# A two-layer diffusion trunk on one core: layer 1's gate brought into columns and spread again through DRAM, and three pieces of side work at other places

## The chip, the cores and the metric

The kernel is one program on one core of a Trainium2 chip. The time is that of the device from the launch to the end, in microseconds (us); lower is better. Beside the times there is one profiled execution, whose trace gives each instruction's start, its length and what it waited for.

## What is computed

A trunk of two layers over 256 latent and 256 context tokens of width 2048. Of the reference, cut to what matters here:

```python
shift, scale, gate = jnp.split(silu_c @ w_mod[l] + b_mod[l], 3, axis=-1)
h    = rmsnorm(x, g_pre[l]) * (1.0 + scale[:, None]) + shift[:, None]
proj = h @ w_in[l]                        # columns: gMLP u, v, gate; q, k, v, gate; Fourier x, gate
y    = mixer_branches(proj, latent_attn, ...)   # 3 branches, 8 attention heads
y    = rmsnorm(y @ w_out[l], g_post[l])
x    = x + gate[:, None] * y              # the context stream likewise, in layer 0 only
```

So each layer has one large projection in, an attention of eight heads and two other mixers, one projection out, and a gate of 2048 values that multiplies the normalised result. The gate is `silu(c) @ w_mod[l][:, 4096:6144] + b_mod`: a vector, of which each value belongs to a column of `y`.

## The kernel before, in words

**Precision and tiling.** All large products are made in halves of fp32: an operand is split into a high part (a cast, on ACT) and the rest (a subtraction, on DVE), and `mm3` (L487 to L490) adds three matmuls, high by high, low by high and high by low. Layer 1's input projection takes two per step (L604, L605). Weights come by `Stream` (L391 to L483): SP loads a piece of 128x1024 into `raw` (3 buffers), ACT casts `whi` (L456, 4 buffers), DVE subtracts `wlo` (L458, 4 buffers), three pieces ahead of their use.

**Stages in order.** Layer 0's modulation and projection; its attention heads and other branches, woven into the projection's columns; the projection out (to about 737 us); the boundary, where the new stream is made; layer 1's projection and attention; and `finish` (L1119 onward), the projection out of layer 1, in four blocks of 512 columns, c = 0 to 3, with 16 k-steps of six matmuls each (two token tiles by three), from about 1030 us.

**What sets the order.** PE's order is written by hand. Side work stands in a list, `Later` (L353 to L377), a clock of its own that each k-step of a product moves on (`later.tick`): a generator that yields 6.0 goes on when the clock has moved by 6.0, and what it then emits comes at that place in PE's order. One k-step of `finish` moves the clock by 1.296, a k-step with 512 columns by 0.648, one of layer 1's projection by 0.324. The orders on DVE, ACT, SP and POOL are the scheduler's; each engine works strictly in its order.

**The gate of layer 1.** `mod_gate1` (L280 to L296) makes the four blocks of 512 values on DVE: each block is an accumulator of 128x512 (tags `ctrh`, `ctrl`, `nstrh`, `nstrl` for c = 0 to 3), to which 16 instructions (L289, L291) add weight rows times a value of `silu(c)`, one per partition. The rows come by SP in loads of 512 KB, two instructions' worth each (L287, tile `mraw`, two buffers). What is left is a sum over the 128 partitions. `gate1(c)` (L298 to L310) does it on PE: two loads on SP bring the block's `b_mod` and `g_post` to all partitions (L302, 256 KB each, into `ws` and `bsb`); ACT and DVE split the accumulator (L505, L506); after `YG` = 6.5 of the clock two matmuls with a matrix of ones leave the sum in all partitions (L307); DVE adds and multiplies (L308, L309). `GATES` (L336) says at which k-step of which column block the task is put in the list. The result is read when a column block of `y` is taken out of PSUM (`evac`, L1170, for c < 3; `close`, L1183, for c = 3), after the block's last matmul.

**The other places.** `mod_four` (L264 to L268) makes four blocks of another modulation vector; its end, `mod_end` (L270 to L278: four small matmuls at L273, then eight small DVE instructions, L150 to L156, into `gg`), is put 45.0 of the clock behind. `x1_of` (L1262 to L1269) makes a block of the new latent stream: a multiplication on DVE and, from the fifth block on, an addition of `x0` by an accumulating DMA on GpSimd's queue; in layer 1's first column blocks it is called `NX` = 4 blocks ahead (L796 to L800). `attention` (L935 to L1003) does `rope` on a head's q (L925 to L927), splits it (L505, L506), and after `YQ` of the clock makes the scores (6.0 in layer 1); then the softmax on ACT and DVE, and after `YA` and `YB` the transposes and the products with v.

Of the kernel before, what the change touches and what calls it, by code (L numbers as in the profile page):

```python
# [7 lines left out]
F32 = mybir.dt.float32  # L8
# [3 lines left out]
ALU = mybir.AluOpType  # L12

P = 128
D = 2048
KT = D // P
# [50 lines left out]
def trunk_kernel(ctx: ExitStack, tc: tile.TileContext, xT, xhalf, cT, wss, wsl, wmod, win, wout0, wout1, const, vec, rows,  # L67
                 wmat, bs, sink, out):
    nc = tc.nc
    V, A, G, PE, DMA = nc.vector, nc.scalar, nc.gpsimd, nc.tensor, nc.sync  # L70

    pool = ctx.enter_context(tc.tile_pool(name="sb", bufs=1))
    psum = ctx.enter_context(tc.tile_pool(name="ps", bufs=1, space=bass.MemoryType.PSUM))
    W2K = 7
    cnt = [0]

    def sb(shape, dt, tag, bufs=1):
        cnt[0] += 1
        return pool.tile(shape, dt, tag=tag, bufs=bufs, name=f"{tag}_{cnt[0]}")

    def w2k(shape, dt=F32):
        return sb(shape, dt, "w2k", W2K)

    def mm_ps(name="mm"):
        cnt[0] += 1
        return psum.tile([P, 512], F32, tag="mm", bufs=6, name=f"ps_{name}_{cnt[0]}")

    def ms_ps(name="ms"):
        cnt[0] += 1
        return psum.tile([P, 512], F32, tag="ms", bufs=2, name=f"ps_{name}_{cnt[0]}")  # L90
# [36 lines left out]
    def cc(name):  # L127
        o, w = COFF[name]
        return cst[:, o - P:o - P + w]

    def vc(l, name):
        o, w = VOFF[name]
        return vecs[:, l, o:o + w]
# [8 lines left out]
    g1 = []  # L142

    def mod_cols(l, cb, ps8):

        what, j0 = cb // 4, (cb % 4) * 4
        b = vc(l, "bmod")[:, cb * 4:cb * 4 + 4].unsqueeze(2).to_broadcast([P, 4, 2])
        sl = slice(j0, j0 + 4)
        if what == 0:
            V.tensor_tensor(out=sh[l][:, sl], in0=ps8, in1=b, op=ALU.add)  # L150
        else:
            dst = (gs[l] if what == 1 else gg0)[:, sl]
            g = vc(l, "gpre" if what == 1 else "gpost")[:, sl].unsqueeze(2).to_broadcast([P, 4, 2])
            V.scalar_tensor_tensor(out=dst, in0=ps8, scalar=1.0 if what == 1 else 0.0, in1=b,
                                   op0=ALU.add, op1=ALU.add)
            V.tensor_tensor(out=dst, in0=dst, in1=g, op=ALU.mult)  # L156
# [83 lines left out]
    def mod_dve(l, cb, red):  # L240

        acc = sb([P, 2, 512], F32, "macc")
        for kg in range(4):
            for kk in range(4):
                if kk % 2 == 0:
                    w = sb([P, 2, 512], F32, "mraw", 2)
                    DMA.dma_start(w, wmod[(cb - 8) if l == 0 else 4 + cb, kg][:, kk:kk + 2])
                for s in range(2):
                    c = cs[:, kg * 4 + kk, s:s + 1]
                    if kg == 0 and kk == 0:  # L250
                        V.tensor_scalar(out=acc[:, s], in0=w[:, kk % 2], scalar1=c, scalar2=None, op0=ALU.mult)
                    else:
                        V.scalar_tensor_tensor(out=acc[:, s], in0=w[:, kk % 2], scalar=c, in1=acc[:, s],  # L253
                                               op0=ALU.mult, op1=ALU.add)
                if kk % 2 and (kg < 3 or kk < 3):
                    yield
        t = sb([P, 2, 512], F32, "mraw", 2)
        for s in range(2):
            V.transpose(t[:, s], acc[:, s])
            V.tensor_reduce(out=red[:, s], in_=t[:, s].rearrange("p (b j) -> p b j", j=32),  # L260
                            axis=mybir.AxisListType.X, op=ALU.add)
        yield

    def mod_four(l, cbs):  # L264
        red = sb([P, 4, 2, 16], F32, "red", 2)
        for i, cb in enumerate(cbs):
            yield from mod_dve(l, cb, red[:, i])
        later.add(mod_end(l, cbs, red), 45.0)  # L268

    def mod_end(l, cbs, red):  # L270
        ps = ms_ps("modc")
        for q in range(4):
            PE.matmul(ps[32 * q:32 * q + 32, 0:32], cc("selq"),  # L273
                      red.rearrange("p c s (j q) -> p c s j q", q=4)[:, :, :, :, q], start=True, stop=True,
                      tile_position=(0, 32 * q))
        for i, cb in enumerate(cbs):
            mod_cols(l, cb, ps[:, 8 * i:8 * i + 8].rearrange("p (s j) -> p j s", s=2))
        yield 0.0  # L278
# [19 lines left out]
    def gate1(c):  # L298

        r = [sb([P, 512], F32, tag) for tag in ("ws", "bsb")]  # L300
        for i in range(2):
            DMA.dma_start(r[i], rows[None, i, c * 512:(c + 1) * 512].to_broadcast([P, 512]))  # L302
        parts = split_into(w2k([P, 512], F32R), w2k([P, 512], F32R), g1[c])
        yield YG
        ps = ms_ps("gate")
        for i, t in enumerate(parts):
            PE.matmul(ps, state["ones"], t, start=i == 0, stop=i == 1)  # L307
        V.tensor_tensor(out=g1[c], in0=r[0], in1=ps, op=ALU.add)  # L308
        V.tensor_tensor(out=g1[c], in0=g1[c], in1=r[1], op=ALU.mult)  # L309
        yield 0.0  # L310

    def mod_rest():
# [21 lines left out]
    LOWC = 60  # L334
    YT = 3.0
    GATES = {2: 0, 14: 1}, {14: 2}, {12: 3}, {}  # L336
    YG = 6.5
    WARM = 4
    YH = 2.0
    NX, LATE = 4, 12  # L340
    YX, YC, YE = [2.4, 1.4, 1.8], 1.5, 5.0
    YQ, YA, YB = [5.5, 6.0], [10.0, 8.6], [3.8, 4.0]

    def pace():

# [31 lines left out]
    later = Later()  # L377
# [126 lines left out]
    def split_into(hi, lo, src):  # L504
        A.copy(hi, src)  # L505
        V.tensor_tensor(out=lo, in0=src, in1=hi.bitcast(F32), op=ALU.subtract)  # L506
        return hi, lo
# [128 lines left out]
    def layer(l):  # L636
# [5 lines left out]
        if last:  # L642
            a = sb([P, 4, 256], F32, "macc")
            c = [sb([P, 2, S], F32, f"kt{j}") for j in range(2)]
# [10 lines left out]
        def take(k, which=(0,)):  # L655

            for i in which:
                if k % (2, 4, 8)[i] == 0:
                    ws_[i] = W.next()

        def start_av(k, ts):
            avw = ws_[0]
            c = slice((k % 2) * 512, (k % 2 + 1) * 512)
            for t in ts:
                sl = slice(t * P, (t + 1) * P)
                mm3(av[t], h_of(l, k, sl), part(avw, c), k == 0, k == KT - 1)
# [129 lines left out]
        for i, (k0, nk) in enumerate(blocks if l else ()):  # L796
            for k in range(k0, k0 + nk):
                made = make_h(1, k, rbs[0], [0])
                if k + NX < KT:
                    x1_of(k + NX)  # L800
            if i == 0:
                with tc.issue_after(made[0].ins), tc.issue_after(made[1].ins):
                    state["late"]()
            take(k0, (0, 1))
            start_av(k0, range(nt))
            if nk == 2:
                start_au(k0)
                start_av(k0 + 1, range(nt))
            start_au(k0 + nk - 1)
# [208 lines left out]
        for h in range(len(au), 4):  # L1018
            ps = tunit1([0])[0] if last else tunit(n)
# [3 lines left out]
        for g in range(4):  # L1023
            ps = tunit1([0])[0] if last else tunit(n)
# [3 lines left out]
        for h in range(4):  # L1028
            ps = tunit1([0])[0] if last else tunit(n)
            gate(h, ps)  # L1030
        state["phase"] = f"cg{l}"
        for g in range(4):
            ps = tunit1([0])[0] if last else tunit(n)
# [24 lines left out]
        for h in range(8):  # L1058
            ps = tunit1([0])[0] if last else tunit(n)
# [3 lines left out]
        for h in range(8):  # L1063
            ps = tunit1([0])[0] if last else tunit(n)
# [69 lines left out]
    def finish():  # L1134
# [68 lines left out]
        for c in range(4):  # L1203
            pss = [mm_ps("y") for _ in range(2)]
            back = BACK if c == 3 else 0
            w = []
            for k in range(KT + back):
                if k < KT:
                    if k % 2 == 0:
                        w.append(W.next())  # L1210
                    products(c, k, 0, pss[0])
                if k == KT - 1:
                    evac(c, 0, pss[0])
                    if c == 3:
                        close(0, pss[0])
                if k >= back:
                    products(c, k - back, 1, pss[1])
                later.tick(PASS * 1024)
                if k in GATES[c]:
                    later.add(gate1(GATES[c][k]))  # L1220
            evac(c, 1, pss[1])
        close(1, pss[1])

# [38 lines left out]
    def x1_of(k):  # L1262

        o = yo[k][:, LAT]
        V.tensor_tensor(out=o, in0=o, in1=state["r0"], op=ALU.mult)
        if k < 4:
            V.tensor_tensor(out=o, in0=o, in1=x0s[0][:, k], op=ALU.add)
        else:
            G.dma_start(o, xhalf[0, k // 4][:, k % 4], accum_op=ALU.add)  # L1269
# [45 lines left out]
    with tc.manual_schedule(engines={EN.PE}):  # L1315
# [12 lines left out]
        for k in range(KT):  # L1328
            q = w2k([P, T])
# [3 lines left out]
            c = slice(32 * (k % 4), 32 * (k % 4) + 32)  # L1333
# [3 lines left out]
        row = w2k([P, T])  # L1337
# [6 lines left out]
        ps = ms_ps("rs")  # L1344
# [16 lines left out]
        make_h(0, 0, rb0, [0, 1], e)  # L1361
        list(e)
        layer(0)
        state["acc"] = out_proj()
        layer(1)
# [78 lines left out]
```

## Time and profile before

| what | value |
|---|---|
| median of 3 runs | 1134.23 us (1133.79 to 1134.24) |
| the profiled execution's own time | 1132.31 us |
| its span, first to last instruction | 1130.5 us |
| busy in the span: PE, DVE, ACT, POOL | 1122.0, 927.6, 528.5, 33.7 us |
| mean granted TensorE clock | 0.999 |

The page gives each engine's busy time, the span in 40 slices, the DMA queues, the chain of work that ended last, the costliest groups of instructions and the DMA issues. A row of a timeline has the start, the length, engine, line, operation, `out<-in` and the tile's shape; what stands in square brackets is the time that the engine stood idle before it, and what released it. Matmuls overlap in PE, so the distance between two starts is read, not their length.

### The profile page before, as it was taken

What the parts mean: (1) busy time and instruction counts of PE and PEld (TensorE: products, weight loads), DVE (VectorE), ACT (ScalarE), POOL (GpSimd) and SP (SyncE); (2) the same over time, 40 slices, a digit from 0 to 9 for tenths busy, and PEclk for the clock granted to TensorE, in tenths of its full rate; (3) what the DMA queues carried; (4) which work ended last, traced back from release to release, by engine and by line L of the source; (5) the groups of instructions that cost most, each with busy time, mean ns of one, the idle gap of its engine ahead of it and who ended that gap; (6) DMA issues with size and microseconds to landing.
All of it is one profiled execution on the core that took longest, in us unless ns stands there. A gap on an engine that the chain in (4) does not pass through costs nothing.

```text
span 1130.5 us, 16656 instructions
## 1 busy us (share of the span) xinstructions
PE 1122.0 (99%) x6117; PEld 921.5 (82%) x6117; DVE 927.6 (82%) x1649; ACT 528.5 (47%) x991; POOL 33.7 (3%) x41
## 2 busy tenths in 40 slices
PE   8999999999999999999999999999999999999998
PEld 3666788888888888888888888988888888888886
DVE  1578799989888788898999988397889789878883
ACT  5322433322235666642533334256665369857551
POOL 0000000000000000000000000030500000000000
PEclk9999999999999999999999999999999999999999
DMA  9999656566656344356556665276956686556972
GB/s 350 403 402 400 243 181 202 170 206 192 215 175 188 107 140 131 122 180 211 186 170 223 221 212 179 94 170 213 226 168 197 214 295 195 158 170 198 315 251 75
DMA packets 75250, 235.85 MB, mean 209 GB/s; under 512 B 8736, under 2 KB 13216, under 8 KB 75168
## 3 DMA queue, kind: packets, MB, share of 16 engines
q1 hardware_dynamic: 70992, 230.85, 61.4%
q0 software_dynamic: 4032, 3.67, 2.2%
q8 instruction: 48, 0.79, 0.3%
q14 instruction: 34, 0.28, 0.1%
q10 hardware_dynamic: 144, 0.26, 0.1%
HBM read 232.65 MB, written 2.10 MB: 208 GB/s over the span
## 4 chain that ended last, share of the span: by engine, by line
PE 96%; DVE 1%; ACT 1%; DMA 0%; issue 0%; SPq 0%; POOLq 0%; DVEq 0%; ACTq 0%
PE ps_t L488 15%; PE ps_t L490 15%; PE ps_t L489 15%; PE ps_t L604 10%; PE ps_t L605 5%; PE ps_v L1053 3%; PE ps_y L488 3%; PE ps_y L490 3%; PE ps_y L489 3%; PE ps_mod L181 2%; PE ps_av L488 2%; PE ps_av L489 2%; PE ps_av L490 2%; PE ps_tp L995 1%; PE ps_v L1054 1%; PE ps_au L488 1%
## 5 line engine op out<-in xcount | busy, mean ns | idle before, releaser
L456 ACT CAST whi<-raw 128x1024 fp32r<-128x1024 f32 (+1 forms) x209 | 216.4, 1037 | 320.6 <-PE ps_t L489 221.9
L488 PE MATMUL ps_t<-hh,whi 128*128 128x512 f32 (+1 forms) x752 | 290.6, 386 | 0.0
L490 PE MATMUL ps_t<-hh,wlo 128*128 128x512 f32 (+1 forms) x752 | 289.7, 385 | 0.0
L489 PE MATMUL ps_t<-hl,whi 128*128 128x512 f32 (+1 forms) x752 | 289.6, 385 | 0.0
L458 DVE TENSOR_TENSOR wlo<-raw,whi 128x1024 fp32r<-128x1024 f32 (+1 forms) x209 | 250.9, 1203 | 45.8 <-ACT whi L456 40.0
L253 DVE SCALAR_TENSOR_TENSOR macc<-mraw,cs,macc 128x512 f32<-128x512 f32 x360 | 250.0, 745 | 11.5 <-DMA mraw<-in_wmod_dram 11.2
L604 PE MATMUL ps_t<-hh,whi 128*128 128x512 f32 x512 | 184.9, 399 | 0.0
L490 PEld LDWEIGHTS ps_t<-hh,wlo 128*128 128x128 f32 x752 | 141.3, 188 | 28.5
L488 PEld LDWEIGHTS ps_t<-hh,whi 128*128 128x128 f32 x752 | 141.3, 188 | 26.9
L489 PEld LDWEIGHTS ps_t<-hl,whi 128*128 128x128 f32 x752 | 141.3, 188 | 26.4
L605 PE MATMUL ps_t<-hh,wlo 128*128 128x256 f32 x512 | 143.4, 280 | 0.0
L604 PEld LDWEIGHTS ps_t<-hh,whi 128*128 128x128 f32 x512 | 96.2, 188 | 21.5
L605 PEld LDWEIGHTS ps_t<-hh,wlo 128*128 128x128 f32 x512 | 96.6, 189 | 0.4
L570 ACT ACTIVATE hh<-w2k,sh 128x256 fp32r<-128x256 f32 x48 | 22.1, 503 | 72.7 <-DVE w2k L566 72.7
L488 PE MATMUL ps_y<-whi,hh 128*128 128x512 f32 x104 | 41.3, 397 | 0.0
L490 PE MATMUL ps_y<-whi,hh 128*128 128x512 f32 x104 | 40.6, 390 | 0.0
L489 PE MATMUL ps_y<-wlo,hh 128*128 128x512 f32 x104 | 40.5, 389 | 0.0
L488 PE MATMUL ps_av<-whi,hh 128*128 128x512 f32 x94 | 39.0, 415 | 0.6 <-ACT hh L570 0.6
L489 PE MATMUL ps_av<-wlo,hh 128*128 128x512 f32 x94 | 37.1, 395 | 0.0
L505 ACT CAST w2k<-ps_tp 128x512 fp32r<-128x512 f32 x40 | 23.4, 586 | 20.3 <-PE ps_scc L489 8.6
L518 POOL TENSOR_TENSOR rs_b<-rs_a,mhalf 128x2 f32<-128x2 f32 (+1 forms) x6 | 6.6, 1096 | 776.8 <-DVE mx L1245 584.8
L506 DVE TENSOR_TENSOR w2k<-ps_tp,w2k 128x512 fp32r<-128x512 f32 x40 | 27.4, 684 | 1.3 <-ACT w2k L505 0.5
(458 smaller groups left out, 1777.0 us busy)
## 6 DMA issues: line engine op xcount, KB each, us to landing
raw<-in_win_dram SPq DMA_DIRECT2D x160, 512.0 KB, 4.1
mraw<-in_wmod_dram SPq DMA_DIRECT2D x128, 512.0 KB, 4.2
raw<-in_wout_dram SPq DMA_DIRECT2D x60, 512.0 KB, 4.4
mraw<-in_wsl_dram SPq DMA_DIRECT2D x14, 512.0 KB, 7.2
yo<-in_xT_dram SPq DMA_DIRECT2D x16, 256.0 KB, 5.3
yo<-in_wsl_dram SPq DMA_DIRECT2D x16, 256.0 KB, 7.2
macc<-in_wsl_dram SPq DMA_DIRECT2D x7, 512.0 KB, 7.7
vv<-in_wsl_dram SPq DMA_DIRECT2D x7, 512.0 KB, 8.4
```

The lines of the kernel that those rows point to most:

```text
L181: PE.matmul(self.ps[32 * kk:32 * kk + 32, 0:self.N], cpad[:, kg * 4 + kk], self.w[kg * 4 + kk], start=kg == 0, stop=kg == 3, tile_position ...
L253: V.scalar_tensor_tensor(out=acc[:, s], in0=w[:, kk % 2], scalar=c, in1=acc[:, s], op0=ALU.mult, op1=ALU.add)
L456: A.copy(ph, rc)
L458: self.last = V.tensor_tensor(out=pl, in0=rc, in1=ph.bitcast(F32), op=ALU.subtract)
L488: PE.matmul(ps, st[0], mv[0], start=start, stop=False)
L489: PE.matmul(ps, st[0], mv[1], start=False, stop=False)
L490: PE.matmul(ps, st[1], mv[0], start=False, stop=stop)
L505: A.copy(hi, src)
L506: V.tensor_tensor(out=lo, in0=src, in1=hi.bitcast(F32), op=ALU.subtract)
L604: PE.matmul(ps, w[0], h, start=k == 0, stop=False)
L605: PE.matmul(ps[:, 0:S], w[1], h[:, 0:S], start=False, stop=k == KT - 1)
L1053: PE.matmul(vps[t], hi, wk, start=k == 0, stop=False)
```

## The change

It has four parts. Blocks 1, 2 and 3 of layer 1's gate go another way (block 0 stays with `gate1`). `MODEND` puts layer 0's `mod_end` 8 of the clock further behind. `AHEADX` makes the calls of `x1_of` run up to two blocks further ahead in layer 1's first steps. `YQ` of layer 1 goes from 6.0 to 6.8.

```diff
-        later.add(mod_end(l, cbs, red), 45.0)
+        later.add(mod_end(l, cbs, red), MODEND[l])
...
         parts = split_into(w2k([P, 512], F32R), w2k([P, 512], F32R), g1[c])
-        yield YG
+        yield YG[0]
...
+    def gate1_dram(c):
+
+        tag = ("ctrh", "ctrl", "nstrh", "nstrl")[c]
+        red, t = sb([P, 16], F32, "red", 2), w2k([P, 512])
+        V.transpose(t, g1[c])
+        V.tensor_reduce(out=red, in_=t.rearrange("p (b j) -> p b j", j=32), axis=mybir.AxisListType.X, op=ALU.add)
+        yield YG[1]
+        ps = ms_ps("gate")
+        for q in range(4):
+            PE.matmul(ps[32 * q:32 * q + 32, 0:4], cc("selq"), red.rearrange("p (j q) -> p j q", q=4)[:, :, q],
+                      start=True, stop=True, tile_position=(0, 32 * q))
+        col = sb([P, 4], F32, "mx", 2)
+        V.tensor_tensor(out=col, in0=ps[:, 0:4], in1=vc(1, "bmod")[:, 32 + 4 * c:36 + 4 * c], op=ALU.add)
+        V.tensor_tensor(out=col, in0=col, in1=vc(1, "gpost")[:, 4 * c:4 * c + 4], op=ALU.mult)
+        row = dram.tile([4, P], F32, tag=f"gate{c}", name=f"gate{c}")
+        with nc.allow_non_contiguous_dma(reason="512 values"):
+            G.dma_start(row.rearrange("j p -> p j"), col)
+        g1[c] = sb([P, 4, P], F32, tag)
+        G.dma_start(g1[c], row[None].to_broadcast([P, 4, P]))
+        g1[c] = g1[c].rearrange("p j f -> p (j f)")
+        yield 0.0
...
-    YG = 6.5
+    YG = 6.5, 3.0
+    MODEND = 53.0, 45.0
     WARM = 4
     YH = 2.0
-    NX, LATE = 4, 12
+    NX, AHEADX, LATE = 4, 2, 12
     YX, YC, YE = [2.4, 1.4, 1.8], 1.5, 5.0
-    YQ, YA, YB = [5.5, 6.0], [10.0, 8.6], [3.8, 4.0]
+    YQ, YA, YB = [5.5, 6.8], [10.0, 8.6], [3.8, 4.0]
...
-                if k + NX < KT:
-                    x1_of(k + NX)
+                for kk in range(min(2 * k, k + AHEADX) + NX, min(2 * k + 2, k + 1 + AHEADX) + NX):
+                    if kk < KT:
+                        x1_of(kk)
...
-                    later.add(gate1(GATES[c][k]))
+                    later.add((gate1_dram if GATES[c][k] else gate1)(GATES[c][k]))
```

The lines of the changed kernel are shifted: its L292 is L291 of before (the accumulation), L482 is L458 (`wlo`), L529 and L530 are L505 and L506 (the splits), L1195 is L1170 (`evac`), L950 to L952 are L925 to L927 (`rope`), L480 is L456 (`whi`).

The first place is on DVE in `finish`, late in column block 1 and at its `evac`, before the change; `nstrl` is block 3's accumulator, `nstrh` block 2's, the `mraw` tiles are the weight rows.

```order
L291 SCALAR_TENSOR_TENSOR nstrl_10269<-mraw_10444,cs_86,nstrl_10269 128x512 x2
L291 SCALAR_TENSOR_TENSOR nstrl_10269<-mraw_10472,cs_86,nstrl_10269 128x512
L458 TENSOR_TENSOR wlo_10531<-raw_10528,whi_10530 128x1024
L1170 TENSOR_TENSOR yo_1956_10547<-ps_y_10355,ctrl_8568 128x512
L506 TENSOR_TENSOR w2k_10559<-nstrh_9229,w2k_10558 128x512
L291 SCALAR_TENSOR_TENSOR nstrl_10269<-mraw_10472,cs_86,nstrl_10269 128x512
L458 TENSOR_TENSOR wlo_10571<-raw_10568,whi_10570 128x1024
L1170 TENSOR_TENSOR yo_1962_10562<-ps_y_10356,ctrl_8568 128x512
```

The same place on DVE with the change, from the fifth load of block 3 (`mraw_10449`) on:

```order
L292 SCALAR_TENSOR_TENSOR nstrl_10271<-mraw_10449,cs_88,nstrl_10271 128x512 x2
L482 TENSOR_TENSOR wlo_10496<-raw_10493,whi_10495 128x1024
L292 SCALAR_TENSOR_TENSOR nstrl_10271<-mraw_10477,cs_88,nstrl_10271 128x512 x2
L482 TENSOR_TENSOR wlo_10514<-raw_10511,whi_10513 128x1024
L292 SCALAR_TENSOR_TENSOR nstrl_10271<-mraw_10517,cs_88,nstrl_10271 128x512 x2
L482 TENSOR_TENSOR wlo_10536<-raw_10533,whi_10535 128x1024
L317 STREAM_TRANSPOSE w2k_10560<-nstrh_9231 128x512
L292 SCALAR_TENSOR_TENSOR nstrl_10271<-mraw_10539,cs_88,nstrl_10271 128x512
L1195 TENSOR_TENSOR yo_1956_10552<-ps_y_10353,ctrl_10409 128x512
L318 TENSOR_REDUCE red_10559<-w2k_10560 128x16
```

Before, the split of `nstrh` stood behind half of block 3's sixth load (`mraw_10472`); now the transposition and the reduction of `nstrh` stand behind block 3's sixth, seventh and half its eighth load (`mraw_10477`, `mraw_10517`, `mraw_10539`).

The second place is on PE: where gate 2's matmuls stand among those of column block 2 is given by the clock, and moves from six k-steps after that block's begin to three. For gate 1, in column block 1, the rows of PE with the change are:

```order
L512 MATMUL ps_y_10353<-whi_10296,hh_1847_10080 128x512
L513 MATMUL ps_y_10353<-wlo_10297,hh_1847_10080 128x512
L514 MATMUL ps_y_10353<-whi_10296,hh_1847_10080 128x512
L512 MATMUL ps_y_10354<-whi_10296,hh_1847_10080 128x512
L513 MATMUL ps_y_10354<-wlo_10297,hh_1847_10080 128x512
L514 MATMUL ps_y_10354<-whi_10296,hh_1847_10080 128x512
L322 MATMUL ps_gate_10399<-red_10345,cst_81 32x4 x4
L512 MATMUL ps_y_10353<-whi_10296,hh_1848_10083 128x512
```

The four small matmuls (32x4) take the place of two of 128x512, 22 rows earlier.

The third place is on DVE in layer 0's attention. Before, `mod_end`'s eight instructions stood ahead of a head's `rope` (L925 to L927) and of its splits (L506):

```order
L971 RECIPROCAL den_3400<-den_3400 128x4
L154 SCALAR_TENSOR_TENSOR gg_31_98<-ps_modc_3474,vecs_78 128x8 x2
L156 TENSOR_TENSOR gg_31_98<-gg_31_98,vecs_78 128x8
L154 SCALAR_TENSOR_TENSOR gg_31_98<-ps_modc_3474,vecs_78 128x8
L156 TENSOR_TENSOR gg_31_98<-gg_31_98,vecs_78 128x8
L154 SCALAR_TENSOR_TENSOR gg_31_98<-ps_modc_3474,vecs_78 128x8
L156 TENSOR_TENSOR gg_31_98<-gg_31_98,vecs_78 128x8
L925 TENSOR_TENSOR w2k_3441<-ps_t_3323,cst_79 128x256
L926 TENSOR_TENSOR mgl_2843<-mgl_2843,cst_79 128x256
```

With the change they stand behind the next head's probabilities, ahead of the head after:

```order
L996 RECIPROCAL den_3532<-den_3532 128x4
L530 TENSOR_TENSOR w2k_3570<-ps_tp_3564,w2k_3569 128x512
L155 SCALAR_TENSOR_TENSOR gg_31_100<-ps_modc_3615,vecs_80 128x8 x2
L157 TENSOR_TENSOR gg_31_100<-gg_31_100,vecs_80 128x8
L155 SCALAR_TENSOR_TENSOR gg_31_100<-ps_modc_3615,vecs_80 128x8
L157 TENSOR_TENSOR gg_31_100<-gg_31_100,vecs_80 128x8
L155 SCALAR_TENSOR_TENSOR gg_31_100<-ps_modc_3615,vecs_80 128x8
L157 TENSOR_TENSOR gg_31_100<-gg_31_100,vecs_80 128x8 x2
L950 TENSOR_TENSOR w2k_3588<-ps_t_3451,cst_81 128x256
```

The same moves on PE: `mod_end`'s four matmuls stand 62 matmuls later than before. On ACT, in layer 1's third head, the cast of q's high part stands behind one `whi` cast before the change (L456, then L505), and behind two with it (L480 twice, then L529).

More of the change, by code (lines that the diff above doesn't have):

```diff
@@ L73, in trunk_kernel @@
     psum = ctx.enter_context(tc.tile_pool(name="ps", bufs=1, space=bass.MemoryType.PSUM))
+    dram = ctx.enter_context(tc.tile_pool(name="dram", bufs=1, space=bass.MemoryType.DRAM))
     W2K = 7
```

## The prediction

> **What bounds the kernel now.** I read the page first: busy time by engine, then the chain that ended last, then the list of what PE waited for.
>
> ```profile
> PE 1122.0 (99%) x6117; PEld 921.5 (82%) x6117; DVE 927.6 (82%) x1649; ACT 528.5 (47%) x991; POOL 33.7 (3%) x41
> PE 96%; DVE 1%; ACT 1%; DMA 0%; issue 0%; SPq 0%; POOLq 0%; DVEq 0%; ACTq 0%
> ```
>
> ```profile
> PE ps_idle L533 <- DVE red L112: 2.0, 1, 2.0
> PE ps_av L488 <- ACT hh L570: 0.6, 1, 0.6
> PE ps_sc L490 <- DVE w2k L506: 0.6, 2, 0.4
> PE ps_x L1194 <- ACT w2k L1186: 0.5, 1, 0.5
> PE ps_rs L1334 <- ACT w2k L1330: 0.3, 1, 0.3
> ```
>
> PE is busy 1122.0 of 1130.5 us and makes up 96% of the chain. So an edit can gain only by taking matmuls away or by removing one of PE's few waits, and it loses by making PE wait. Of the waits listed the change can touch one: the scores (`ps_sc`), twice. The first, third, fourth and fifth are the start of the program and of its stages, and the tail. The two places of the scores, in PE's timeline:
>
> ```profile
> 371.95 0.60 PE L995 MATMUL ps_tp<-identr,w2k 128*128 128x128 f32 x4
> 372.63 0.50 PE L488 MATMUL ps_sc<-kt,w2k 128*128 128x512 f32 x1
> ...
> 373.56 0.50 PE L490 MATMUL ps_sc<-kt,w2k 128*128 128x512 f32 x1 [0.19 <-DVE w2k L506]
> 373.90 0.39 PE L488 MATMUL ps_sc<-kt,w2k 128*128 128x512 f32 x1
> ...
> 936.19 0.39 PE L489 MATMUL ps_sc<-ws,w2k 128*128 128x512 f32 x1
> 936.96 0.50 PE L490 MATMUL ps_sc<-kt,w2k 128*128 128x512 f32 x1 [0.38 <-DVE w2k L506]
> ```
>
> A 128x512 matmul in a row of them takes 0.23 us of PE (the chain's row at 1043.35, below). From 372.63 to 373.90 three intervals take 1.27, 0.58 too much; the four transposes ahead take 0.68, where the four of the row at 1042.92 take 0.44, so 0.24 too much. Together 0.8 us in layer 0. In layer 1 one interval of 0.77 is 0.54 too long.
>
> **The change, part by part.**
>
> *Layer 0's `mod_end`, 8 of the clock later.* Why the scores waited:
>
> ```profile
> 369.91 0.24 DVE L154 SCALAR_TENSOR_TENSOR gg<-ps_modc,vecs 128x8 f32<-128x8 f32 x2 [3.44 <-PE ps_modc L273]
> ...
> 385.13 0.43 DVE L925 TENSOR_TENSOR w2k<-ps_t,cst 128x256 f32<-128x256 f32 x1 [2.97 <-ACT mgl L923]
> ```
>
> DVE stood 3.44 us until PE had made `mod_end`'s sums, and the head's `rope` and splits queued behind. With the change that wait is gone, and `mod_end`'s eight small instructions come about 12 us later, into DVE's idle 2.97 us before 385.13, where nothing is delayed. What is late next: the high half on ACT, which now comes as early as its own copies allow. I take the whole gain, -0.8 us; the bounds are -0.8 and, if ACT and DVE in the next heads, whose order moves too, make one score wait as long as layer 1's does, -0.8 + 0.5 = -0.3.
>
> *Layer 1's scores at 6.8.* The scores stand two steps of the projection later, 6 matmuls or 0.69 us by the pace above. But the order on ACT changes as well: two `whi` casts, not one, stand before the cast of q's high half.
>
> ```profile
> 933.94 1.05 ACT L456 CAST whi<-raw 128x1024 fp32r<-128x1024 f32 x1
> 935.39 0.41 ACT L505 CAST w2k<-mgl 128x256 fp32r<-128x256 f32 x1 [0.41 <-DVE mgl L927]
> ```
>
> A cast takes 1.05, and the second needs the weight buffer that PE frees at about 935.9. So the high half is ready at 935.9 + 1.05 + 0.41 = 937.4, not 935.8, while PE asks at 935.93 + 0.69 = 936.6: a wait of 0.8 where there was 0.54. Against this, DVE's low half (L506, which ended the old wait) has 0.69 more. I take 0.0; bounds -0.5 (the wait gone) and +0.8 (one more such wait in a later head, since the whole chain of a head shifts by two steps).
>
> *`AHEADX`.* The same multiplications and transfers, some earlier.
>
> ```profile
> 738.30 7.37 POOL L1269 DMA_DIRECT2D yo<-in_xhalf_dram  x8 [4.02 <-DVE w2k L566]
> ```
>
> POOL issues the first eight transfers in one run, 0.92 us each, so its own pace sets when they land; earlier calls on DVE don't bring them forward by much. PE shows no wait at that place. 0.0; bounds -0.3 and +0.3, a third of one issue each way.
>
> *Gates on PE.* Three times two 128x512 matmuls go and four small ones (eight in the trace) come.
>
> ```profile
> 1044.34 0.39 PE L490 MATMUL ps_y<-whi,hh 128*128 128x512 f32 x1
> 1044.57 0.62 PE L307 MATMUL ps_gate<-w2k,join 128*128 128x512 f32 x2
> 1045.03 0.40 PE L488 MATMUL ps_y<-whi,hh 128*128 128x512 f32 x1
> ...
> 130.65 0.40 PE L490 MATMUL ps_av<-whi,hl 128*128 128x512 f32 x1
> 130.97 0.24 PE L193 MATMUL ps_modc<-w2k,cst 128*32 128x4 f32 x8
> 131.15 0.50 PE L488 MATMUL ps_au<-hh,whi 128*128 128x512 f32 x1
> 131.49 0.40 PE L489 MATMUL ps_au<-hl,whi 128*128 128x512 f32 x1
> ```
>
> ```profile
> 1042.92 0.44 PE ps_x L1147 x4
> 1043.35 0.23 PE ps_y L488
> ```
>
> The old pair costs 1045.03 - 1044.34 - 0.23 = 0.46 us. The small group of the same shape (32x4) at 130.97 stretches the two intervals around it from 0.46 to 0.84: 0.38 us. So a gate saves 0.08, three save 0.24. I take -0.2. The removed ACT casts and DVE work lie beside PE and gain nothing by themselves.
>
> *Gate 2's place.* This is the main term. PE comes to gate 2's matmuls three k-steps after column block 2 begins, 18 matmuls, and no longer six.
>
> ```profile
> 1077.82 0.39 PE L488 MATMUL ps_y<-whi,hh 128*128 128x512 f32 x1
> ...
> 1085.98 0.63 PE L307 MATMUL ps_gate<-w2k,join 128*128 128x512 f32 x2
> ```
>
> With 1077.82 as the block's begin that is 1077.82 + 18 x 0.2275 = 1081.9. What it needs is DVE's reduction of `nstrh` (L318). In DVE's new order that stands behind block 3's loads up to the first half of the eighth, P7 (P0 to P7 are the loads of `mraw` for that block). Before, half of P5 was enough. DVE works in order, so the reduction can't be done before P7 has landed, and with two buffers P7 is asked for only when P5 is used up, P5 when P3, P3 when P1.
>
> ```profile
> 1061.55 0.74 DVE L291 SCALAR_TENSOR_TENSOR nstrl<-mraw,cs,nstrl 128x512 f32<-128x512 f32 x1
> ...
> 1063.34 0.74 DVE L291 SCALAR_TENSOR_TENSOR nstrl<-mraw,cs,nstrl 128x512 f32<-128x512 f32 x1
> ...
> 1083.00 0.68 DVE L1170 TENSOR_TENSOR yo<-ps_y,ctrl 128x512 f32<-128x512 f32 x1
> 1083.60 1.22 DVE L458 TENSOR_TENSOR wlo<-raw,whi 128x1024 fp32r<-128x1024 f32 x1
> ...
> 1086.88 0.75 DVE L291 SCALAR_TENSOR_TENSOR nstrl<-mraw,cs,nstrl 128x512 f32<-128x512 f32 x1 [0.61 <-DMA mraw<-in_wmod_dram]
> ```
>
> ```profile
> q1 hardware_dynamic: 4396, 14.93, 89.3%
> ...
> mraw<-in_wmod_dram SPq DMA_DIRECT2D x10, 512.0 KB, 5.4
> ```
>
> The last fence is the DMA view of 1040 to 1090: the 16 engines are 89.3% busy there, and a load of `mraw` takes 5.4 us to land. Before, the two rows at 1061.55 and 1063.34 are P1, used up at 1064.0; without the longer additions of gate 1 ahead I put it at 1063.3. Then P7 lands three landings and two uses (2 x 0.7 each) later: 1063.3 + 3 x (5.4 + 0.1) + 2 x 1.4 = 1082.6. Behind it stand half of P7 (0.67), `evac` (0.60, from 1083.00 to 1083.60) and the reduction, which I put at the 0.60 that a 512-wide instruction takes there: 1084.5. **PE waits 1084.5 - 1081.9 = 2.6 us.** Queued behind it is all of block 2. The bounds: with 4.2 us per landing, the page's median for `mraw`, P7 lands at 1079.0 and nothing waits;
>
> ```profile
> mraw<-in_wmod_dram SPq DMA_DIRECT2D x128, 512.0 KB, 4.2
> ```
>
> at before's pace P7 is only there at 1086.88 (the row above is its first half), the reduction ends at 1088.8, and PE waits 6.9. I choose 5.4, the value of this very stage: two row loads leave the queues, but two loads of weights must come sooner.
>
> Gates 1 and 3 I cost at nothing. Gate 1's reduction stands behind fewer loads and, by the same rows, about 1 us ahead of PE's place (1058.8), a margin that one late load can take; gate 3's accumulator is complete some 10 us ahead of its place.
>
> *The way through DRAM.* DVE's two tiny instructions, a transfer of 512 single values out and one of 256 KB back. It is read at `evac`, 20 us or more after the matmuls for blocks 1 and 2. For block 3 there is less, since it is read at `close`:
>
> ```profile
> 1102.78 0.63 PE L307 MATMUL ps_gate<-w2k,join 128*128 128x512 f32 x2
> ...
> 1117.52 0.68 DVE L1183 TENSOR_TENSOR yo<-ps_y,nstrl 128x512 f32<-128x512 f32 x1
> ```
>
> That is 14.7 us from the old place, and the new one is some k-steps ahead of it: 17 us. The nearest row for the transfers is `x0`'s transfers on the same queue; two, one after another, each as long as the whole run of eight at 738.30 (7.4 us), are 15 us. That is covered. If the cover were gone, `evac` would come late, but PE has a second pair of accumulators to go on with, and the cost shows only at the last block. 0; bounds 0 and +3.2, for what its packets take from the loads:
>
> ```profile
> q0 software_dynamic: 4032, 3.67, 2.2%
> ```
>
> This row of the page gives 0.022 x 16 x 1130.5 / 4032 = 0.099 us of an engine per packet; 512 packets are 51 us of one engine or 3.2 us of all sixteen, and they come when P2 or P3 is on its way. A rule of the Trainium skill speaks against the change here: by "DMA: Bandwidth & Descriptors", section "Rules for kernel authors", a strided transfer becomes one descriptor per element. By that the write has 512 packets and costs as said, +3.2 at most; no run here shows it yet.
>
> **Sum, against the profiled execution:** -0.8 + 0.0 + 0.0 - 0.2 + 2.6 = +1.6 us, so 1132.3 + 1.6 = 1133.9. The profiled execution lies 1.9 us below the median of the runs; I add the difference to the median: 1134.2 + 1.6 = **1135.8 us**.
>
> **The rivals.**
>
> *No wait at gate 2 (faster side).* The loads land in 4.2 to 4.7 us, since four rows' loads less are in the way. At 4.7, P7 lands at 1080.5 and the wait is 0.5. For it: the 89.3% includes those rows. Against: no load of the stage landed under 4.7. Total: -0.8 - 0.2 = -1.0, and with layer 1's wait gone as well -1.5: 1132.7. Only with a gain at `AHEADX` or beside it does it pass -2.3.
>
> *The chain of loads is slower (slower side).* The 512 packets and the denser loads add 3.2 us before P7: PE waits 5.8 at gate 2, up to the 6.9 of before's pace. Total +4.8: 1139.0. It passes +2.3 from a wait of 3.3 at gate 2 on, a mean landing of 5.6 us.
>
> *The scores don't gain.* The later places move the waits without removing them (-0.3 and +0.8 in place of -0.8 and 0.0): +2.9, 1137.1.
>
> *The change doesn't do what it says.* The gates were to relieve PE and don't: 0.24 us. That is already in the sum.
>
> **How the numbers follow.** Chances: the forecast (a wait of 1 to 4 us at gate 2) 0.47; no wait 0.23; slower loads 0.20; scores without gain 0.10. The range reaches from the end of the second case with a little more, 1132.0, to 1139.8, that is the third case with its wait at 6.6. About 0.2%, 2.3 us, is what a measurement of this kernel can tell from no change. Faster by more than that needs the second case and a gain that I can't name: 0.11. Slower by more than 1136.5 are the third case, two thirds of the fourth, and the upper third of the forecast: 0.42. The rest, 0.47, lies within.
>
> **What would show it.** Right: PE's list of waits shows `ps_gate` behind DVE's `red` at 1081.9, 1 to 4 us, once; DVE idles ahead of it for `mraw`; the scores near 372 start 0.23 apart; `ps_sc` near 937 still waits 0.5 or more, for ACT. Wrong: no wait of `ps_gate`, a wait for weights (`wlo`) in `finish`, one at `evac` for the transfer back, or new waits of the scores in layer 0's heads from 398 on.

## The result and the profile after

The change made the kernel slower: 1146.39 us (1143.9 to 1147.59, 4 runs) beside 1134.01, a ratio of 1.0106, interval 1.0094 to 1.0118. The forecast was 1135.8, and the range ended at 1139.8. The profiled execution took 1146.76 us with a span of 1145.0, where before had 1132.31 and 1130.5.

PE's waits in the changed kernel, the longest first (us in total, times, longest):

```profile
PE ps_gate L322 <- DVE red L318: 5.2, 1, 5.2
PE ps_y L513 <- DVE wlo L482: 4.1, 1, 4.1
PE ps_idle L557 <- DVE red L113: 2.0, 1, 2.0
PE ps_x L1219 <- ACT w2k L1211: 1.7, 1, 1.7
PE ps_av L512 <- ACT hh L594: 0.6, 1, 0.6
PE ps_sc L512 <- ACT w2k L529: 0.4, 1, 0.4
```

The first wait is the one that was forecast, twice as long. The second, for weights in `finish`, is one that the prediction named as a sign that it is wrong, and the fourth has grown by 1.2. Matching PE's rows of both traces one by one shows where the time goes. At 1074.81 the changed kernel lies 0.3 us **ahead**. At the second matmul of column block 2 it lies 5.7 behind, ten matmuls past gate 2 13.2 behind, at the last product 13.3; the tail adds 1.2, and that is the 14.5 of the spans. PE's timeline at the two places:

```profile
1074.81 0.39 PE L512 MATMUL ps_y<-whi,hh 128*128 128x512 f32 x1
1079.30 0.50 PE L513 MATMUL ps_y<-wlo,hh 128*128 128x512 f32 x1 [4.11 <-DVE wlo L482]
...
1080.37 0.63 PE L514 MATMUL ps_y<-whi,hh 128*128 128x512 f32 x1
1080.80 0.63 PE L512 MATMUL ps_y<-whi,hh 128*128 128x512 f32 x1
...
1087.40 0.39 PE L514 MATMUL ps_y<-whi,hh 128*128 128x512 f32 x1
1092.96 0.29 PE L322 MATMUL ps_gate<-red,cst 128*32 128x4 f32 x8 [5.17 <-DVE red L318]
...
1094.20 0.63 PE L514 MATMUL ps_y<-whi,hh 128*128 128x512 f32 x1
1094.62 0.63 PE L512 MATMUL ps_y<-whi,hh 128*128 128x512 f32 x1
```

Behind each wait the starts lie 0.43 us apart instead of 0.23, for some 3 us. The windows show it as clock: in this view (us, busy time and count of PE, PEld, DVE, ACT and POOL, granted clock, DMA share, GB/s) the third number from the end is 0.66 and 0.57 around those places and 1.00 between.

```profile
1079.00:1084.00 5.00, 4.70 (x14) 3.70 (x15) 4.51 (x7) 1.05 (x1) 0.00 (x0) 0.66 0.86 278
1084.00:1088.00 4.00, 3.79 (x17) 2.80 (x15) 2.88 (x4) 1.05 (x1) 0.00 (x0) 1.00 0.92 292
...
1093.00:1098.00 5.00, 5.00 (x21) 3.99 (x22) 4.89 (x8) 1.35 (x2) 0.76 (x1) 0.57 0.44 143
```

What PE waited for goes back to loads. DVE's and GpSimd's timelines, and the DMA view of 1060 to 1068 (issues with their median time to landing):

```profile
1076.57 1.54 DVE L292 SCALAR_TENSOR_TENSOR nstrl<-mraw,cs,nstrl 128x512 f32<-128x512 f32 x2 [10.04 <-DMA mraw<-in_wmod_dram]
...
1092.13 0.68 DVE L318 TENSOR_REDUCE red<-w2k 128x16 f32<-128x512 f32 x1
...
1134.90 0.69 DVE L1208 TENSOR_TENSOR yo<-ps_y,nstrl 128x512 f32<-128x512 f32 x1 [3.98 <-DMA nstrl<-gate]
```

```profile
1061.85 0.83 POOL L329 DMA_DIRECT2D gate<-mx  x1 [230.41 <-DVE mx L326]
...
1120.50 0.76 POOL L329 DMA_DIRECT2D gate<-mx  x1 [12.41 <-DVE mx L326]
1129.72 0.54 POOL L331 DMA_DIRECT2D nstrl<-gate  x1 [8.46 <-DMA gate<-mx]
```

```profile
raw<-in_wout_dram SPq DMA_DIRECT2D x3, 512.0 KB, 13.8
mraw<-in_wmod_dram SPq DMA_DIRECT2D x2, 512.0 KB, 13.8
gate<-mx POOLq DMA_DIRECT2D x1, 2.0 KB, 10.8
```

In the same columns as above, the stretches behind that write, and then two of them before the change:

```profile
1066.00:1070.00 4.00, 4.00 (x21) 3.34 (x20) 0.53 (x1) 0.00 (x0) 0.00 (x0) 1.00 0.59 15
1070.00:1074.00 4.00, 4.00 (x19) 3.30 (x19) 0.00 (x0) 2.57 (x4) 0.56 (x1) 1.00 0.73 25
```

```profile
1066.00:1070.00 4.00, 4.00 (x21) 3.32 (x20) 4.00 (x6) 2.72 (x5) 0.00 (x0) 1.00 0.83 292
1070.00:1074.00 4.00, 4.00 (x20) 3.30 (x19) 3.96 (x6) 1.96 (x2) 0.00 (x0) 1.00 0.95 352
```

The write of 2 KB issued at 1061.85 took 10.8 us to land, and loads issued beside it took 13.8 where the loads of `mraw` took 5.4 before. For 8 us only 15 to 25 GB/s were moved, where the same stretches moved 292 to 352 before, although the DMA engines count as busy for 0.59 and 0.73 of the time: the packets on their way lasted longer. DVE stood 10.04 us for one of them, and all `wlo` and the reduction stood behind. The third write, when nothing else was on its way, still took 8.9 us (issued at 1120.50), and so gate 3's values came 4 us after DVE wanted them.

### The profile page after: what moved, and what is told of

Same layout as the page of the kernel before. It is cut to its first block, busy times and chain, and to the rows that moved or that the text cites. A ratio compares the mean times of both kernels' runs of the same rounds, so it can differ in the third digit from the quotient of the medians.

```text
span 1145.0 us, 16700 instructions
## 1 busy us (share of the span) xinstructions
PE 1125.8 (98%) x6132; PEld 923.1 (81%) x6135; DVE 926.0 (81%) x1652; ACT 525.6 (46%) x988; POOL 37.7 (3%) x47
## 5 line engine op out<-in xcount | busy, mean ns | idle before, releaser
L480 ACT CAST whi<-raw 128x1024 fp32r<-128x1024 f32 (+1 forms) x209 | 216.0, 1037 | 333.9 <-PE ps_t L513 221.7
L482 DVE TENSOR_TENSOR wlo<-raw,whi 128x1024 fp32r<-128x1024 f32 (+1 forms) x209 | 250.8, 1204 | 55.0 <-ACT whi L480 48.6
L512 PE MATMUL ps_y<-whi,hh 128*128 128x512 f32 x104 | 43.1, 415 | 0.0
L514 PE MATMUL ps_y<-whi,hh 128*128 128x512 f32 x104 | 42.1, 405 | 0.0
L529 ACT CAST w2k<-ps_tp 128x512 fp32r<-128x512 f32 x40 | 23.3, 584 | 19.7 <-PE ps_tp L1020 6.9
L530 DVE TENSOR_TENSOR w2k<-ps_tp,w2k 128x512 fp32r<-128x512 f32 x40 | 27.4, 684 | 2.7 <-ACT w2k L529 1.8
```

The costliest lines, as they stand in the source:

```text
L480: A.copy(ph, rc)
L482: self.last = V.tensor_tensor(out=pl, in0=rc, in1=ph.bitcast(F32), op=ALU.subtract)
L512: PE.matmul(ps, st[0], mv[0], start=start, stop=False)
L514: PE.matmul(ps, st[1], mv[0], start=False, stop=stop)
```

## The experiments

Two theories. **W**: the write of 512 single values is slow in itself and holds back the other transfers. **O**: it is the order, DVE's reduction behind block 3's loads, as the prediction had it, only slower.

**The gates undone, and the gates alone.**

```diff
-    YG = 6.5, 3.0
+    YG = 6.5, 6.5
...
-                    later.add((gate1_dram if GATES[c][k] else gate1)(GATES[c][k]))
+                    later.add(gate1(GATES[c][k]))
```

> The change with all four blocks of the gate made the old way (gate1, 6.5), so that only MODEND, AHEADX and YQ are left. Both theories (the write of 512 single values holds back all other transfers; or DVE's order puts gate 2's reduction behind block 3's loads) leave nothing of the loss here: PE's timeline of the changed kernel lay 0.2 us ahead of before's until the projection out of layer 1, so 1133.8 against 1134.0. Above 1135 a part of the loss would come from elsewhere.

Measured 1132.18 beside 1133.64, ratio 0.9988 (0.9979 to 0.9997): the other three parts gain a little. The interval only just excludes no change, and the two profiled executions (1132.35, and 1132.31 before) don't show the gain.

```diff
-    MODEND = 53.0, 45.0
+    MODEND = 45.0, 45.0
-    NX, AHEADX, LATE = 4, 2, 12
+    NX, AHEADX, LATE = 4, 0, 12
-    YQ, YA, YB = [5.5, 6.8], [10.0, 8.6], [3.8, 4.0]
+    YQ, YA, YB = [5.5, 6.0], [10.0, 8.6], [3.8, 4.0]
```

> Only the gates go the new way; MODEND, AHEADX and YQ as before. Both theories: all of the loss, 1146.4 + 0.2 = 1146.6. If the moved work mattered for the loss, under 1144.

Measured 1145.77, ratio 1.0112 (1.0096 to 1.0127). The gates are the whole loss.

**The write alone**, in before's kernel:

```diff
         V.tensor_tensor(out=g1[c], in0=g1[c], in1=r[1], op=ALU.mult)
+        if c:
+            row = dram.tile([4, P], F32, tag=f"gate{c}", name=f"gate{c}")
+            with nc.allow_non_contiguous_dma(reason="512 values"):
+                G.dma_start(row.rearrange("j p -> p j"), g1[c][:, 0:4])
         yield 0.0
```

> Before's kernel with one thing added: after each of gates 1, 2 and 3, GpSimd's queue writes 512 single values of the gate to DRAM; nobody reads them. Theory W (the write holds all other transfers for some 10 us): the loads that are issued next to a write land in 10 to 14 us where they took 5, PE waits for wlo, and the time is 3 to 9 us longer, 1137 to 1143. Theory O (DVE's order): the DVE order is before's, so within 0.5 us of 1134.0.

Measured 1144.67, ratio 1.0097 (1.0084 to 1.0111). DMA view of 1069 to 1081 in that kernel, then its waits of PE:

```profile
raw<-in_wout_dram SPq DMA_DIRECT2D x3, 512.0 KB, 11.9
mraw<-in_wmod_dram SPq DMA_DIRECT2D x2, 512.0 KB, 11.7
bsb<-in_rows_dram SPq DMA_DIRECT2D x1, 256.0 KB, 5.9
gate<-ctrl POOLq DMA_DIRECT2D x1, 2.0 KB, 11.6
```

```profile
PE ps_y L494 <- DVE wlo L463: 3.3, 1, 3.3
PE ps_y L493 <- ACT hl L461: 2.8, 1, 2.8
```

Three writes of 2 KB that nobody reads cost 11 us, with before's order on every compute engine; that is more than the 3 to 9 that I expected under W. O falls as the main cause.

**Runs of 16 bytes**, in the changed kernel: the four values of a partition side by side. The read follows the write's layout, so each value ends in another column than it belongs to; the amount of work is the same, and so is the order on DVE and ACT.

```diff
-        row = dram.tile([4, P], F32, tag=f"gate{c}", name=f"gate{c}")
+        row = dram.tile([P, 4], F32, tag=f"gate{c}", name=f"gate{c}")
...
-            G.dma_start(row.rearrange("j p -> p j"), col)
+            G.dma_start(row, col)
...
-        G.dma_start(g1[c], row[None].to_broadcast([P, 4, P]))
+        G.dma_start(g1[c].rearrange("p j f -> p (j f)").rearrange("p (f j) -> p f j", j=4), row[None].to_broadcast([P, P, 4]))
```

> The changed kernel with the write laid out as 128 runs of 16 bytes instead of 512 single values; the gate's values then land in other columns. The DVE order is that of the change. Theory W, with the time of the write set by its number of runs: it lands in 2 to 5 us instead of 10, and of the 12.4 us lost 2 to 5 are left: 1136 to 1139. If any write to DRAM from this queue held the others, or under theory O: 1145 to 1147.

Measured 1138.11, ratio 1.0039 (1.0025 to 1.0052). With idle engines the write took 1.7 us (view of 1108 to 1114); what is left of the loss, 4 of the 12 us, is O's. Views in this order: the issue, PE's wait, DVE's timeline, two windows.

```profile
gate<-mx POOLq DMA_DIRECT2D x1, 2.0 KB, 1.7
```

```profile
PE ps_gate L322 <- DVE red L318: 3.0, 1, 3.0
```

```profile
1083.56 0.75 DVE L292 SCALAR_TENSOR_TENSOR nstrl<-mraw,cs,nstrl 128x512 f32<-128x512 f32 x1 [0.21 <-DMA mraw<-in_wmod_dram]
1084.23 0.68 DVE L1195 TENSOR_TENSOR yo<-ps_y,ctrl 128x512 f32<-128x512 f32 x1
1084.83 0.68 DVE L318 TENSOR_REDUCE red<-w2k 128x16 f32<-128x512 f32 x1
```

```profile
1086.00:1092.00 6.00, 6.00 (x15) 4.75 (x16) 5.89 (x10) 1.12 (x2) 0.55 (x1) 0.52 0.55 187
1092.00:1098.00 6.00, 6.00 (x28) 4.96 (x27) 3.37 (x4) 2.10 (x2) 0.54 (x1) 1.00 0.70 137
```

P7 is there at 1083.56 and the reduction ends at 1085.5: the chain of the prediction, 1 us late. But the wait of 3.0 us costs 6.1: PE lies 0.6 behind before at its start, and 6.7 behind 14 matmuls later, since those run at a clock of 0.52.

The same, with the gate matmuls back at 6.5 (`YG = 6.5, 6.5`):

> Runs of 16 bytes (values in other columns), and PE's gate matmuls back at 6.5 of the clock. With 16-byte runs at 3.0, PE waited 3.0 us at gate 2 and then ran some 13 matmuls at 0.43 instead of 0.23 us, 6 us in all. If that wait and the slow clock behind it are all that was left: 1138.1 - 6 = 1132.1. If the chain of loads behind the DVE order also delays weights, or the transfers still cost: 1134 to 1137.

Measured 1132.33, ratio 0.9990 (0.9981 to 0.9999). The wait and the clock behind it were all that was left.

**The same write on ACT's hardware queue.**

```diff
-            G.dma_start(row.rearrange("j p -> p j"), col)
+            nc.scalar.dma_start(row.rearrange("j p -> p j"), col)
```

> The changed kernel, the write of 512 single values issued on ACT's hardware queue instead of GpSimd's. If what holds the other transfers is the 512 single runs: the write still lands in 9 to 11 us, PE's waits for wlo and at gate 2 stay, 1143 to 1148. If it is GpSimd's way of making descriptors: the write lands in 2 to 4 us and the time is that of 16-byte runs or better, 1136 to 1139.

Measured 1142.57, ratio 1.0080 (1.0065 to 1.0095). The DMA view of 1092 to 1104:

```profile
q10 hardware_dynamic: 528, 0.00, 2.5%
...
raw<-in_wout_dram SPq DMA_DIRECT2D x5, 512.0 KB, 8.1
gate<-mx ACTq DMA_DIRECT2D x1, 2.0 KB, 10.2
```

10.2 us from this queue too: it is not GpSimd's queue. The 528 packets show that the write does go out value by value. The third write met idle engines: issued at 1116.88, it landed at 1126.99. Its packets in the view of 1117.7 to 1118.2, and its landing in the view of 1116 to 1128:

```profile
q10 hardware_dynamic: 528, 0.00, 50.5%
```

```profile
gate<-mx ACTq DMA_DIRECT2D x1, 2.0 KB, 10.1
```

All its packets lie within half a microsecond, and the landing comes 8.8 us after the last of them. So the time doesn't go into sending 512 packets.

**Is it the number of runs, their length, or their distance?** Before's kernel with the writes alone, in other layouts: 512 runs of 64 bytes; 512 single values 128, 64, 32 and 16 bytes apart, with one partition's four values as neighbours; and 16 and 64 bytes apart in the change's order, where the neighbours belong to other partitions. The diff is that of the single values with one partition's four as neighbours (`f` is 32, 16, 8 or 4); in the change's order the tile is `[4, P, f]`, and the runs of 64 bytes fill 16 of 32 places from 64 columns of `g1[c]`.

```diff
-            row = dram.tile([4, P], F32, tag=f"gate{c}", name=f"gate{c}")
+            row = dram.tile([P, 4, f], F32, tag=f"gate{c}", name=f"gate{c}")
...
-                G.dma_start(row.rearrange("j p -> p j"), g1[c][:, 0:4])
+                G.dma_start(row[:, :, 0:1], g1[c][:, 0:4].rearrange("p (j f) -> p j f", f=1))
```

> As the kernel with the writes alone, but each of the 512 runs is 64 bytes long (to places 128 bytes apart), sixteen times the bytes. If the number of runs sets how long the write lasts and holds the others: it lands in 9 to 12 us and the time is 1142 to 1146. If it is that a run is shorter than some granule of the memory: it lands in 3 to 6 us and the time is 1134 to 1138.

> As the kernel with the writes alone, 512 single values, but each to a place of its own, 128 bytes from the next, so that no two engines write side by side. If the collisions of neighbours are what lasts: landing in 2 to 6 us, 1134 to 1138. If each single run costs: landing in 9 to 12 us, 1142 to 1146.

> 512 single values 64 bytes apart. A stretch of 64 bytes or less: as 128 apart, 2.2 us with idle engines, 5 under load, 1133.6. Longer than 64: 3 to 6 us.

> 512 single values 32 bytes apart. A stretch of 64 bytes: 2 values in each, landing in 3 to 6 us, 1133.5 to 1135. A stretch of 32 or less: as 128 apart, 2.2 us with idle engines, 1133.6.

> As the writes alone, 512 single values 16 bytes apart. If the collision is between values in one stretch of 64 bytes (4 of them here instead of 16): shorter than 10 us, 4 to 7, and 1134 to 1138. If the stretch is 16 bytes or less: 2 to 5 us and 1133.6.

> Writes alone, the change's order of the 512 single values (neighbours from other partitions), 16 bytes apart. If it is whose neighbours they are, within 64 bytes (4 partitions in each): landing in 4 to 7 us even with idle engines, 1135 to 1139. If the distance alone counts: 3.0 us with idle engines as in the run with one partition's values 16 bytes apart, 1134.4.

> The same order, 64 bytes apart. If sharing a stretch of 64 bytes or less is what costs: 2.2 us with idle engines, 1133.5. If the order of the values itself (consecutive partitions to rows far apart) costs: 9 us and 1144.

| 512 runs, each | order | landing with idle engines | time, ratio to before |
|---|---|---|---|
| 4 B, side by side | the change's | 9.3 us | 1144.67, 1.0097 |
| 4 B, 16 B apart | the change's | 2.5 us | 1133.78, 1.0006 (0.9994 to 1.0017) |
| 4 B, 64 B apart | the change's | 2.2 us | 1133.73, 1.0001 (0.9989 to 1.0012) |
| 4 B, 16 B apart | a partition's together | 3.0 us | 1134.42, 1.0010 (0.9999 to 1.0022) |
| 4 B, 32 B apart | a partition's together | 2.6 us | 1134.06, 1.0000 (0.9989 to 1.0011) |
| 4 B, 64 B apart | a partition's together | 2.2 us | 1133.36, 1.0002 (0.9991 to 1.0014) |
| 4 B, 128 B apart | a partition's together | 2.2 us | 1133.59, 0.9999 (0.9990 to 1.0009) |
| 64 B, to places 128 B apart | a partition's together | 2.1 us | 1134.44, 1.0010 (1.0001 to 1.0019) |

The rows behind the table's first two lines: the second and third write side by side, of which the third met idle engines, and the third write 16 bytes apart in the same order.

```profile
gate<-nstrh POOLq DMA_DIRECT2D x1, 2.0 KB, 11.2
...
gate<-nstrl POOLq DMA_DIRECT2D x1, 2.0 KB, 9.3
```

```profile
gate<-nstrl POOLq DMA_DIRECT2D x1, 2.0 KB, 2.5
```

The number of runs costs next to nothing: 512 single values land in 2.2 us when they lie 64 bytes apart. The first two writes, beside loads, took 4.3 to 6.8 us in all layouts below the table's first line. My theory W had the right culprit and the wrong reason; what costs is that single values are written side by side. Runs of 16 bytes side by side don't cost it: 1.7 us. Whose neighbours the values are makes little difference at 16 bytes (2.5 and 3.0 us); side by side only the change's order was tried, and no distance between 4 and 16 bytes. Of each write on GpSimd's queue the trace keeps 32 packets: the last of the third write lies 7.6 us ahead of the landing side by side, 0.8 us at 16 bytes in the same order. Why single values side by side are so late to land and stop the loads, these runs don't show.

**A version that computes everything and avoids the single values.** The 128x4 is turned into 4x128 by one more PE transposition; the write is then 4 runs of 512 bytes, and the gates stand at 6.5.

```diff
-        row = dram.tile([4, P], F32, tag=f"gate{c}", name=f"gate{c}")
-        with nc.allow_non_contiguous_dma(reason="512 values"):
-            G.dma_start(row.rearrange("j p -> p j"), col)
+        yield 1.2
+        ps = ms_ps("gate")
+        PE.transpose(ps[0:4, 0:P], col, ident)
+        flat = w2k([P, P])
+        V.tensor_copy(out=flat[0:4, :], in_=ps[0:4, 0:P])
+        row = dram.tile([4, P], F32, tag=f"gate{c}", name=f"gate{c}")
+        G.dma_start(row, flat[0:4, :])
```

> The whole computation, with the gate's 128x4 turned by one more PE transposition into 4x128, so that the write is 4 runs of 512 bytes, and the gate matmuls at 6.5. Both remedies: three more transpositions of about 0.3 us, less 0.2 us saved on the gates: 1132.2 + 0.8 = 1133.0. If writes to DRAM from this queue hold others whatever their runs: above 1136.

Measured 1137.3, ratio 1.0032 (1.0021 to 1.0044): a miss. One k-step was too little for DVE, whose two small instructions stand behind loads of block 3, and PE waited again:

```profile
PE ps_gate L329 <- DVE mx L326: 3.8, 2, 3.1
```

With 3.9 in place of 1.2 for blocks 1 and 2:

> As the kernel with 4 runs of 512 bytes, whose transposition made PE wait 3.1 + 0.7 us for DVE's two small instructions; here it stands 3.9 of the clock behind the gate matmuls (1.2 still for block 3). Expected: no wait at ps_gate, 1132.2 + 0.8 = 1133.0; if another wait takes its place, 1135 to 1138.

Measured 1134.22, ratio 1.0008 (0.9999 to 1.0017). The wait is down to 0.2 us, and nothing is gained over the gates undone: their ratio was 0.9988, so this kernel is about 2 us slower than they are, 0.8 of it expected for the transpositions. Where the rest goes is open; the profiled execution, 1132.27 us, doesn't show it.

**The parts that were moved.** `MODEND` alone (53.0 for layer 0) and `YQ` alone (6.8 for layer 1), each in before's kernel:

> Before's kernel with MODEND alone. By the prediction -0.8, 1133.2 (beside 1134.0); by PE's timeline of the changed kernel, where the scores of layer 0 still wait 0.7 us (now for ACT's cast of the probabilities), -0.1, 1133.9. The trace tells it better than the time: PE's excess between 371 and 374.

> Before's kernel with YQ of layer 1 at 6.8 alone. By the prediction 0.0 (a wait of 0.8 for ACT in place of 0.54 for DVE); by PE's timeline of the changed kernel, where the scores near 937 start at the normal distances, -0.5 us: 1133.0 beside 1133.5.

Measured 1132.52, ratio 0.9993 (0.9985 to 1.0002), and 1132.79, ratio 0.9994 (0.9985 to 1.0003). Neither time is clear of no change, so the traces decide. PE's timeline with `MODEND` alone:

```profile
371.11 0.60 PE L995 MATMUL ps_tp<-identr,w2k 128*128 128x128 f32 x4
372.11 0.51 PE L488 MATMUL ps_sc<-kt,w2k 128*128 128x512 f32 x1 [0.40 <-ACT w2k L505]
372.45 0.40 PE L489 MATMUL ps_sc<-ws,w2k 128*128 128x512 f32 x1
372.69 0.39 PE L490 MATMUL ps_sc<-kt,w2k 128*128 128x512 f32 x1
```

And with `YQ` alone:

```profile
936.59 0.39 PE L488 MATMUL ps_sc<-kt,w2k 128*128 128x512 f32 x1
936.82 0.40 PE L489 MATMUL ps_sc<-ws,w2k 128*128 128x512 f32 x1
937.05 0.43 PE L490 MATMUL ps_sc<-kt,w2k 128*128 128x512 f32 x1
937.33 0.39 PE L488 MATMUL ps_sc<-kt,w2k 128*128 128x512 f32 x1
```

## Why the prediction was wrong, step by step

- **The step that failed** is "The way through DRAM", put at 0 with +3.2 as its end. It took the write's price from the mean of 0.099 us per packet, spread over sixteen engines, and the landing from `x0`'s transfers of 128 KB. Measured, the write alone costs 11 us in before's kernel, and 8.3 of the 10.6 us by which the forecast missed go when only its layout changes (1146.4 to 1138.1). It lasts 9 to 11.6 us, and meanwhile loads take 11.7 to 13.8 us (medians); no row of before showed a write of single values side by side. The cover that I named, 20 us for blocks 1 and 2, was cover for the gate's own landing. It was none for the loads beside it.
- **The Trainium skill's rule** that I weighed ("DMA: Bandwidth & Descriptors", "Rules for kernel authors": one descriptor per element) gave the right number of packets, 528 on the hardware queue, and pointed against the change. But the packets were not the price: spread out, as many cost 2.2 us and no time.
- **Gate 2's place** was right in mechanism: a wait of PE for `red`, behind P7. With runs of 16 bytes it is 3.0 us against 2.6 forecast, P7 at 1083.56 against 1082.6, and the three landings on the way to P7 take 5.9, 5.7 and 4.9 us where 5.4 each were taken.
- **What a wait costs** was missing in the sum. I counted the 2.6 us alone; PE ran some 14 matmuls at half clock behind it, and 3.0 us of waiting cost 6.1. With 6.1 in place of 2.6 the forecast would have been 1135.8 + 3.5 = 1139.3, beside the 1138.1 measured with 16-byte runs.
- **`close`**: 17 us of cover were named for block 3, and there were 17.1 (PE's gate matmuls at 1113.79, DVE free at 1130.92). The trip was put at 15 us and took 14.4 (8.9, 5.2 and the gap); that is luck, since each part was put at 7.4. What I missed is the start. In DVE's order the two small instructions of gate 3 stood behind `evac` of block 2 (at 1118.48), so the write was issued at 1120.50, 6.7 us after PE's matmuls, and DVE was 4.0 us late. With runs of 16 bytes and the same order it is issued 1.9 us after them (1107.20 and 1109.10): the rest of the delay came from weights that landed late beside the second write, for which ACT stood 6.3 and 2.9 us. I took the start of the trip from PE's place, not from DVE's row.
- **`mod_end`**: -0.8 forecast, -0.1 measured in PE's timeline. The wait for DVE went, but 0.56 us of the 1.00 between 371.11 and 372.11 are now lost to ACT's cast, the next one late (four transposes take 0.44 in the prediction's row). I had named ACT's high half as what is late next, and given it no time.
- **`YQ`**: 0.0 forecast; the 0.54 us are gone, the four rows above stand 0.23 to 0.28 apart. The second `whi` cast did no harm: it ran right behind the first and q's cast began at 935.87, so it didn't have to wait for the buffer that I let it wait for.
- **`AHEADX`** and the gates' 0.24 us of PE: nothing in the traces contradicts them. Gate 1's exchange gains 0.09 us in PE's rows, 0.08 forecast. No run tried `AHEADX` alone.
- **Two slips of counting** change no term. Two steps of layer 1's projection are four matmuls, not six; their 0.69 us are right. And the scores are the third in the list of waits, so the starts of stages and the tail are the first, second, fourth and fifth.

## What to carry to other kernels

A transfer's price is also what it does to the transfers beside it: ask how its runs lie in memory, and try it alone in the old kernel, unread, before anything is built on it. In these runs a wait on TensorE of 2.5 us or more cost 1.7 to 3.1 us beyond its own length; count that too. The start of a chain that leaves an engine is that engine's row in its own order, not the place where the work was asked for.

## What the hardware showed that was not expected

- 512 values of 4 bytes written side by side to DRAM take 8.9 to 10.1 us with idle engines and 9.5 to 11.6 beside loads, from either queue, though on ACT's queue, with idle engines, all packets are out within half a microsecond. The core's other loads nearly stop: 15 to 25 GB/s are moved between 1066 and 1074 of the changed kernel, where the kernel before moved 292 to 352, and 27 to 40 beside the second write of the write-alone kernel (1104 to 1111). At 16 bytes' distance the write takes 2.5 to 3.0 us, at 64 or more 2.2, and the loads go on (4.4 us, median of the weights' loads beside the second write in the kernel with 16 bytes in the change's order).
- After a wait of 2.5 to 5.2 us 128x512 matmuls start 0.43 us apart, and the trace's granted clock is 0.50 for 3.4 or 6.8 us, begun within the wait or up to 1.5 us behind it; 2.5 us is the shortest such wait, in the kernel with the write on ACT's queue. After waits of up to 1.3 us (at 763, in the kernel with 32 bytes) they don't. The Trainium skill, "TensorE: Matmul & The Clock Gate", "Part 1: The HAM clock gate", says that an idle window of about 3.4 us halves the clock, and a busy one restores it; its cold step for 512 columns is 0.427 us. The step agrees with the measured 0.43, and so do the lengths; but here waits shorter than 3.4 us were enough.
